# A trunk kernel's stick-breaking attention: beta stays in PSUM, the mask becomes a matmul, and GpSimd takes subtractions

## The chip, the cores and the metric

The kernel runs as one program on one core of a Trainium2 chip. The metric is the device time of one execution in microseconds (us). The engines are named as the profile names them: PE is TensorE's matmuls and PEld its weight loads, DVE is VectorE, ACT is ScalarE, POOL is GpSimd, SP is SyncE, which issues the DMAs. "L582" is line 582 of the kernel before.

## What is computed

A trunk of two layers over 1024 frames of width 1024, in float32. Layer 0 mixes stick-breaking attention (8 heads of 64) and a pooling mixer, layer 1 is gated linear attention, and each is followed by a gated MLP with a causal convolution of width 3. The change touches layer 0's attention and what surrounds it:

```python
def even_mixer(h, w_in, q_gain, k_gain, pool_w, pool_scale, w_out):
    proj = h @ w_in
    q, k, v, xb = jnp.split(proj, [SB_WIDTH, 2 * SB_WIDTH, 3 * SB_WIDTH], axis=-1)
    q = rms_norm(q.reshape(b, s, SB_HEADS, SB_HEAD_DIM), q_gain)
    k = rms_norm(k.reshape(b, s, SB_HEADS, SB_HEAD_DIM), k_gain)
    o_a = stick_breaking_attention(q, k, v)
    o_b = multiscale_pool(xb, pool_w, pool_scale)
    return jnp.concatenate([o_a, o_b], axis=-1) @ w_out

# stick_breaking_attention: A[t,s] = beta_ts * prod_{s<j<t}(1 - beta_tj), s < t
    z = einsum(q_blk, kh) * dh ** -0.5
    visible = key_pos < q_pos
    log_fail = where(visible, log_sigmoid(-z), 0)
    later = (cumulative sum of log_fail from the right, without the element itself)
    weights = where(visible, exp(log_sigmoid(z) + later), 0)
    out = weights @ v
```

So with beta = sigmoid(z), a weight is beta times the product of (1 - beta) over all later visible keys.

## The kernel before

Activations lie transposed, 128 features by 1024 frames to a tile. Every float32 operand of a matmul is split into a rounded part hi (fp32r, made by ScalarE's copy) and a rest lo (fp32r, made by a subtraction); `mm3` (L122) then does hi x hi, hi x lo and lo x hi. So every tile costs a ScalarE copy and a subtraction before TensorE can use it: `load_split` (L102) for weights, with the subtraction on VectorE or, with `eng=G`, on GpSimd; `stack` (L443) for a head's q and k; `pool_out` (L487, ph and pl) and `split_h` (L509, mh and ml) for what goes into the output projection.

**Attention.** For each of 4 pairs p of heads, each head a, and each block i of 128 queries, the keys up to the diagonal are cut into chunks of 512: one *unit* is a block of queries against one chunk, of 128, 256, 384 or 512 columns. The unit with the diagonal comes first, and its neighbour to the left continues its product. 96 units in all, 64 with the diagonal. A unit goes through these steps:

- `scores` (L558): two matmuls (L562, L563) put z into a PSUM bank "z". ScalarE makes pt = sigmoid(-z), that is 1 - beta (L567), and bt = beta (L569), both into SBUF. In a diagonal unit GpSimd sets the column after the last to 1 (L571), and two selects (L573) set the masked part of the last 128 columns of pt to 1 and of bt to 0.
- `weights` (L576): VectorE runs a multiplying scan over pt from right to left (L582; its second operator is a bypass, so what stands as the second input is read and not used), and multiplies bt by pt moved by one (L584).
- `transpose` (L586): TensorE transposes bt, 128 columns at a time (L590), into a bank "t"; ScalarE and VectorE empty it into the parts hi (L598) and lo (L599).
- `outputs` (L601), once per two blocks of queries: matmuls with the values (L609, L611) into a bank "d", which ScalarE (L614) and VectorE (L617) empty.

**Order.** TensorE's order is written out by hand (L664 to L695). Step s issues the scores of unit s+2, the weights of unit s+1, and the transposes of unit s. Between them a `Filler` (L143) issues other matmuls, by a planned time per column (`seg`, `RATES`): projections of the next pair's q and k (`qk_prep`, L365), pooling (`pool_in`, `pool_out`), values, and last, in segment (3,0), the first part of the output projection (`out_first`, L519). A generator that yields None ends the current fill, so that a few steps pass before its next matmul. `out_first` splits the six inputs listed in `first`, with two None each, and then multiplies with all six. The queues of the other engines are ordered by the framework, which plans with a model of its own, and then run strictly in that order. At the start of each segment `stack` prepares the head that comes one segment later; for the first two heads it runs right before the attention.

**PSUM.** Eight banks: two each for the names lin (projections), z, t and d, taken in turns. `qk_prep` puts the statistics of q and k (L376) and two transposed row scales (L431) into d.

## Time and profile before

| | us |
|---|---|
| median of 3 runs (2330.53 to 2331.79) | 2330.87 |
| the profiled execution | 2332.11 |
| its span, first to last instruction | 2330.1 |
| PE busy in it | 2230.3 (96%) |
| DVE busy | 1691.2 (73%) |
| ACT busy | 1024.7 (44%) |
| POOL busy | 468.6 (20%) |

Section 2 of the page cuts the span into 40 slices and gives each engine's busy share in tenths; PEclk is the clock granted to TensorE, where 9 stands for 90% or more. In a list of waits, a row reads: the engine and line that waited, the engine and line that released it, total us, times, longest us. In a list of one line's instructions the three numbers are the shortest, median and longest in ns. In a timeline a row gives start and duration in us, and in brackets the idle time before it and what ended it; "x4" is four merged instructions. Matmul durations overlap, so TensorE's pace is read from the distance of their starts.

The attention stage runs from about 66 to 452 us. The first MLP follows it.

### The profile page before, as it was taken

How to read it: one execution, taken by the hardware profiler on the slowest of the kernel's cores; microseconds unless marked ns; L12 is line 12 of the kernel's file. 1: busy time of each engine (PE TensorE's matmuls, PEld its weight loads, DVE VectorE, ACT ScalarE, POOL GpSimd, SP SyncE). 2: the span in 40 equal slices, each digit the busy share in tenths (PEclk: the TensorE clock that was granted, in tenths of full speed). 3: DMA queues.
4: the chain of work that ended last, by engine and by line, in shares of the span. 5: the costliest groups of instructions: out<-in, count | busy, mean ns of one | idle time of the engine just before them, and what ended most of it. 6: DMA issues, size and time to landing. Idle time of an engine off the chain costs nothing.

```text
span 2330.1 us, 27466 instructions
## 1 busy us (share of the span) xinstructions
PE 2230.3 (96%) x10560; PEld 1832.4 (79%) x10560; DVE 1691.2 (73%) x2236; ACT 1024.7 (44%) x1492; POOL 468.6 (20%) x422
## 2 busy tenths in 40 slices
PE   8989988989999999999998999999899999999999
PEld 7778767767888887888886888787688888878887
DVE  5687797698999998744445545557999999986543
ACT  6556665464444444312146343627544444442210
POOL 1352462041111111422020000003211111124210
PEclk9999989999999999999999999999899999999999
DMA  4001112222222224522001111112122222254211
GB/s 140 19 19 31 38 32 101 68 100 64 82 84 82 84 85 137 204 103 91 10 23 43 37 37 37 46 38 90 64 89 84 82 82 82 82 199 163 92 53 73
DMA packets 51427, 178.53 MB, mean 77 GB/s; under 512 B 5968, under 2 KB 6608, under 8 KB 51296
## 3 DMA queue, kind: packets, MB, share of 16 engines
q1 hardware_dynamic: 51296, 176.78, 23.0%
q8 instruction: 83, 1.36, 0.2%
q14 instruction: 48, 0.39, 0.1%
HBM read 140.06 MB, written 36.70 MB: 76 GB/s over the span
## 4 chain that ended last, share of the span: by engine, by line
PE 80%; DVE 11%; ACT 4%; issue 3%; DMA 1%; POOL 1%; SPq 0%; DVEq 0%; POOLq 0%; ACTq 0%
PE lin L783 15%; PE z L783 10%; PE lin L127 5%; PE lin L129 5%; PE t L783 5%; PE d L783 5%; PE lin L131 5%; PE z L127 2%; PE z L129 2%; PE z L131 2%; PE t L127 2%; PE t L129 2%; PE t L131 2%; PE d L129 2%; PE d L127 2%
## 5 line engine op out<-in xcount | busy, mean ns | idle before, releaser
L113 ACT CAST whi<-wraw 128x1024 fp32r<-128x1024 f32 (+4 forms) x108 | 107.5, 997 | 359.2 <-PE d L129 229.3
L941 POOL TENSOR_TENSOR c<-c 128x1024 f32<-128x1024 f32 x44 | 108.1, 2458 | 756.4 <-ACT c L940 756.4
L801 DVE TENSOR_TENSOR u<-u,rstd_bc 128x512 f32<-128x512 f32 x168 | 167.1, 996 | 2.8
L114 DVE TENSOR_TENSOR wlo<-wraw,whi 128x1024 fp32r<-128x1024 f32 (+3 forms) x96 | 138.0, 1438 | 40.5 <-ACT whi L113 39.6
L970 POOL TENSOR_TENSOR act<-a,act 128x1024 fp32r<-128x1024 f32 x40 | 107.8, 2703 | 217.7 <-ACT act L969 210.8
L846 ACT ACTIVATE c<-u,prm 128x1024 f32<-128x1024 f32 x88 | 109.3, 1245 | 84.8 <-DVE u L801 73.8
L582 DVE TENSOR_TENSOR_SCAN pt<-pt 128x128 f32<-128x128 f32 (+3 forms) x96 | 99.9, 1041 | 37.9 <-POOL pt L573 28.6
L127 PE MATMUL lin<-h_hi,whi 128*128 128x512 f32 x304 | 119.6, 432 | 7.0 <-ACT whi L113 7.0
L783 PE MATMUL d<-T,a 128*128 128x512 f32 x504 | 121.1, 389 | 0.0
L849 DVE SCALAR_TENSOR_TENSOR c<-u,prm,c 128x1022 f32<-128x1022 f32 x88 | 115.3, 1312 | 0.1
L847 DVE SCALAR_TENSOR_TENSOR c<-u,prm,c 128x1023 f32<-128x1023 f32 x88 | 112.3, 1278 | 2.8 <-ACT c L846 2.7
L722 DVE TENSOR_TENSOR x<-x,t 128x512 f32<-128x512 f32 x97 | 66.4, 684 | 66.1 <-PE t L131 66.0
L129 PE MATMUL lin<-h_lo,whi 128*128 128x512 f32 x304 | 112.3, 407 | 0.3
L131 PE MATMUL lin<-h_hi,wlo 128*128 128x512 f32 x304 | 111.5, 406 | 0.0
L783 PE MATMUL lin<-T,s12h 128*128 128x512 f32 x336 | 105.8, 396 | 5.8 <-ACT tm L816 5.8
L783 PEld LDWEIGHTS d<-T,a 128*128 128x128 f32 x504 | 94.6, 188 | 19.6
L762 ACT CAST s12h<-s 128x1024 fp32r<-128x1024 f32 x42 | 44.2, 1053 | 146.1 <-PE lin L783 146.1
L783 PE MATMUL z<-blk,s34h 128*128 128x512 f32 x336 | 105.7, 395 | 2.8 <-DVE u L832 2.8
L722 DVE TENSOR_TENSOR x<-x,d 128x512 f32<-128x512 f32 x97 | 66.3, 684 | 56.8 <-PE d L131 56.7
L783 PE MATMUL lin<-blk,whi 128*128 128x512 f32 x336 | 106.6, 399 | 0.0
L783 PE MATMUL z<-blk,s12h 128*128 128x512 f32 x336 | 105.8, 396 | 0.0
L783 PE MATMUL t<-blk,whi 128*128 128x512 f32 x336 | 103.7, 390 | 0.0
(388 smaller groups left out, 6526.7 us busy)
## 6 DMA issues: line engine op xcount, KB each, us to landing
wraw<-in_wup SPq DMA_DIRECT2D x46, 512.0 KB, 3.6
act<-c SPq DMA_DIRECT2D x44, 512.0 KB, 2.6
wraw<-in_wdn SPq DMA_DIRECT2D x44, 512.0 KB, 3.7
raw_g<-in_wup SPq DMA_DIRECT2D x42, 512.0 KB, 3.6
a<-act SPq DMA_DIRECT2D x40, 512.0 KB, 4.4
xs<-x SPq DMA_DIRECT2D x16, 512.0 KB, 2.6
x<-xs SPq DMA_DIRECT2D x16, 512.0 KB, 5.0
x<-in_xT SPq DMA_DIRECT2D x8, 512.0 KB, 6.0
```

The lines of the kernel that those rows point to most:

```text
L114: (eng or V).tensor_tensor(lo[:, cs], raw[:, cs], hi[:, cs].bitcast(F32), op=ALU.subtract)
L127: PE.matmul(out[i], wh, ah[i], start=first, stop=False)
L129: PE.matmul(out[i], wh, al[i], start=False, stop=False)
L131: PE.matmul(out[i], wl, ah[i], start=False, stop=last)
L722: V.tensor_tensor(x[m][:, cs], x[m][:, cs], pss[i], op=ALU.add)
L783: PE.matmul(ps, w, m, start=first and k == 0 and n == 0, stop=k == 3 and n == 2, skip_group_check=True)
L801: V.tensor_tensor(dst, dst, rstd_bc[:, cs], op=ALU.mult)
L846: S.activation(c, u, AF.Identity, scale=pcol(b + 2), bias=pcol(b + 3))
L847: V.scalar_tensor_tensor(c[:, 1:], u[:, :T - 1], pcol(b + 1), c[:, 1:], op0=ALU.mult, op1=ALU.add)
L849: V.scalar_tensor_tensor(c[:, 2:], u[:, :T - 2], pcol(b), c[:, 2:], op0=ALU.mult, op1=ALU.add)
L941: G.tensor_tensor(ca, ca, cg, op=ALU.mult)
L970: G.tensor_tensor(t[1], a32, t[0].bitcast(F32), op=ALU.subtract)
```

## The change

- **PSUM banks.** One name per bank, and a table says which use takes which banks in turn. Outside the attention it is as before, two for each of lin, z, t, d. During the attention z has three and d one. `qk_prep`'s statistics and row scales use t instead of d, except for the first pair's, before the attention.
- **Mask.** Two constants are made at the start: minus 1e30 on a diagonal, and a triangle of ones. In a diagonal unit a third matmul adds their product to the last 128 columns of z; the sigmoids then give 1 and 0 there. The two selects and the memset on GpSimd go; ScalarE copies the 1 into pt's extra column.
- **beta in PSUM.** The second sigmoid writes over z in its bank. The scan's second, unused input is now that bank, and the product reads beta from it and writes bt anew in SBUF (2 buffers instead of 3).
- **Subtractions.** VectorE's subtractions in `stack` (kl, qs), `pool_out` (pl) and `split_h` (two loaded and all but the last computed input) go to GpSimd.

```diff
-    psum = ctx.enter_context(tc.tile_pool(name="psum", bufs=2, space=PSUM))
+    psum = ctx.enter_context(tc.tile_pool(name="psum", bufs=1, space=PSUM))
...
+    turns = {}
+
+    def share_out(**uses):
+        turns.clear()
+        turns.update({u: itertools.cycle(b) for u, b in uses.items()})
+
     def bank(tag):
-        return psum.tile([P, 512], F32, tag=tag, name=tag)
+        return psum.tile([P, 512], F32, tag=f"bank{next(turns[tag])}", name=tag)
+
+    share_out(lin=(0, 1), z=(2, 3), t=(4, 5), d=(6, 7))
...
+    tri = etile("pw", F32, 528)[:, 0:P]
+    G.affine_select(out=tri, in_=ones, compare_op=ALU.is_ge, fill=0.0,
+                    base=0, pattern=[[1, P]], channel_multiplier=-1)
+    S.copy(later, tri)
+    S.activation(nbig, ident, AF.Copy, scale=-MASK)
...
-            st = bank("d")
+            st = bank("t" if start is None else "d")
...
-            bc = bank("d")
+            bc = bank("t" if start is None else "d")
...
-        V.tensor_sub(kl[r], kg[r], kh[r].bitcast(F32))
-        V.tensor_sub(qs[o], qg[r], qs[r].bitcast(F32))
+        G.tensor_tensor(kl[r], kg[r], kh[r].bitcast(F32), op=ALU.subtract)
+        G.tensor_tensor(qs[o], qg[r], qs[r].bitcast(F32), op=ALU.subtract)
...
-            V.tensor_sub(pl, ob[:, cs], ph.bitcast(F32))
+            G.tensor_tensor(pl, ob[:, cs], ph.bitcast(F32), op=ALU.subtract)
...
-            return load_split(o_d[k - NPAIR], hpool, ("h", "h"), nb=16)
+            return load_split(o_d[k - NPAIR], hpool, ("h", "h"), nb=16, eng=G)
...
-        V.tensor_sub(ml, src, mh.bitcast(F32))
+        (V if k == NPAIR - 1 else G).tensor_tensor(ml, src, mh.bitcast(F32), op=ALU.subtract)
...
-        z = bank("z")[:, 0:u.n]
+        n, first_ = u.n, u.above is None
+        u.z = z = bank("z")[:, 0:n]
...
-        PE.matmul(z, lq, kl[:, u.k0:u.k1], start=False, stop=True)
+        PE.matmul(z, lq, kl[:, u.k0:u.k1], start=False, stop=not first_)
+        if first_:
+            PE.matmul(z[:, n - P:n], nbig, later, start=False, stop=True)
...
-        u.bt = bt = etile("bt", F32, 512, 3)
-        S.activation(bt[:, 0:n], z, AF.Sigmoid, scale=qsc[:, 0, col:col + 1])
-        if u.above is None:
-            G.memset(pt[:, n:n + 1], 1.0)
-            for d_, fill in ((pt[:, n - P:n], 1.0), (bt[:, n - P:n], 0.0)):
-                G.affine_select(out=d_, in_=d_, compare_op=ALU.is_gt, fill=fill,
-                                base=0, pattern=[[-1, P]], channel_multiplier=1)
+        if first_:
+            S.copy(pt[:, n:n + 1], ones[:, 0:1])
+
+        S.activation(z, z, AF.Sigmoid, scale=qsc[:, 0, col:col + 1])
...
-        V.tensor_tensor_scan(pr, pr, pr, 1.0 if first_ else u.above.pt[:, 0:1],
+        V.tensor_tensor_scan(pr, pr, z[:, ::-1], 1.0 if first_ else u.above.pt[:, 0:1],
                              op0=ALU.mult, op1=ALU.bypass)
-        V.tensor_tensor(bt[:, 0:n], bt[:, 0:n], pt[:, 1:n + 1], op=ALU.mult)
+        u.bt = etile("bt", F32, 512, 2)
+        V.tensor_tensor(u.bt[:, 0:n], z, pt[:, 1:n + 1], op=ALU.mult)
...
+    share_out(lin=(0, 1), z=(2, 3, 6), t=(4, 5), d=(7,))
...
+    share_out(lin=(0, 1), z=(2, 3), t=(4, 5), d=(6, 7))
```

The last two lines stand right before and right after the attention's loop.

## The prediction

> **What bounds the kernel now.** I read the page's slices first, to find where TensorE is not full; then busy times by stage; then what TensorE waited for in the two bad stages; then one stall instruction by instruction.

> ```profile
> PE   8989988989999999999998999999899999999999
> ...
> DVE  5687797698999998744445545557999999986543
> ...
> PEclk9999989999999999999999999999899999999999
> ```
> One slice is 58.3 us. TensorE is full nearly everywhere; the change touches only the attention stage, slices 2 to 8 (about 64 to 455 us), where PE drops to 8 three times, the clock to 8 once, and VectorE (DVE) rises to 9 there. What lies behind 460 us keeps its instructions, so the sum concerns these stages:

> ```profile
> 64.00:76.00 12.00, 7.38 (x22) 5.54 (x21) 5.05 (x6) 5.28 (x10) 7.71 (x11) 0.72 0.00 0
> 76.00:320.00 244.00, 225.90 (x1319) 193.98 (x1318) 190.23 (x325) 157.41 (x306) 99.18 (x169) 0.97 0.09 28
> 320.00:390.00 70.00, 54.04 (x243) 44.25 (x242) 62.01 (x85) 39.06 (x69) 34.58 (x48) 0.83 0.26 90
> 390.00:452.00 62.00, 62.00 (x328) 52.39 (x328) 41.18 (x65) 26.30 (x50) 7.93 (x22) 1.00 0.16 50
> ```
> The columns are stretch, length, busy time of PE, PEld, DVE, ACT, POOL, granted clock, DMA share and GB/s. In 76 to 320 TensorE idles 244.0 - 225.9 = 18.1 us, and a clock of 0.97 costs 225.9 x 0.03 = 6.8 us more. In 320 to 390 it idles 16.0 us and the clock costs 54.0 x 0.17 = 9.2 us. From 390 to 452 it idles not at all: nothing can be won there except by less TensorE work. What TensorE waited for, first in 76 to 320, then in 320 to 390 (total, times, longest):

> ```profile
> PE t L590 <- DVE atl L599: 7.5, 2, 3.8
> PE d L611 <- DVE atl L599: 3.4, 4, 2.0
> ```
> ```profile
> PE d L611 <- DVE atl L599: 9.2, 4, 4.0
> PE t L590 <- DVE atl L599: 5.5, 2, 4.5
> ```
> So 10.9 of 18.1 us, and 14.7 of 16.0 us, end when VectorE's L599 has emptied a transpose bank. VectorE is late, not slow by itself; one such stall shows why (GpSimd, VectorE, TensorE):

> ```profile
> 153.88 2.51 POOL L114 TENSOR_TENSOR wlo<-wraw,whi 128x1024 fp32r<-128x1024 f32 x1
> ```
> ```profile
> 152.91 1.28 DVE L584 TENSOR_TENSOR bt<-bt,pt 128x512 f32<-128x512 f32 x1
> 154.22 3.25 DVE L451 TENSOR_TENSOR qs<-qg,qs 64x1024 fp32r<-64x1024 f32 x1
> 157.50 0.69 DVE L599 TENSOR_TENSOR atl<-t,ath 128x512 fp32r<-128x512 f32 x1
> ```
> ```profile
> 158.25 1.12 PE L590 MATMUL t<-ident,bt 128*128 128x128 f32 x4 [3.82 <-DVE atl L599]
> ```
> L451 stands ahead of the urgent L599 in VectorE's queue. It starts at 154.22, GpSimd's subtraction ends at 156.39, and 1.08 us later L451 is done: it got through only after GpSimd. TensorE lost 3.82 us.

> **The change part by part.** Which VectorE instructions does GpSimd stretch? Shortest, median and longest in ns:

> ```profile
> L584 DVE TENSOR_TENSOR bt<-bt,pt x96: 270/680/1522, 71.7 to 430.9; 128x512 f32<-128x512 f32 x48, 128x128 f32<-128x128 f32 x16, 128x256 f32<-128x256 f32 x16, 128x384 f32<-128x384 f32 x16
> ```
> ```profile
> L582 DVE TENSOR_TENSOR_SCAN pt<-pt x96: 417/1210/2285, 71.1 to 429.5; 128x512 f32<-128x512 f32 x48, 128x128 f32<-128x128 f32 x16, 128x256 f32<-128x256 f32 x16, 128x384 f32<-128x384 f32 x16
> ```
> ```profile
> L494 DVE TENSOR_TENSOR pl<-o_b,ph x8: 658/666/1518, 141.4 to 382.6; 128x512 fp32r<-128x512 f32 x8
> ```
> ```profile
> L464 DVE TENSOR_TENSOR o_b<-lin,rstd_bc x8: 659/674/692, 115.3 to 333.4; 128x512 f32<-128x512 f32 x8
> ```
> L494, with both inputs in SBUF, reaches 1518 ns; L464, with one in PSUM, never passes 692. The scan and the product become of L464's kind, so I take them at their short durations, never stretched. Reading PSUM costs 674 - 666 = 8 ns by these rows, under 2 us over 192 instructions.

> [...] The two rows above show 8 ns, and I go by them.

> VectorE also loses the subtractions. GpSimd's work by rows:

> ```profile
> L573 POOL TENSOR_SCALAR_AFFINE_SELECT bt<-bt 128x128 f32<-128x128 f32 x64 | 37.6, 588 | 4.7 <-ACT bt L569 4.2
> L573 POOL TENSOR_SCALAR_AFFINE_SELECT pt<-pt 128x128 f32<-128x128 f32 x64 | 30.7, 480 | 138.1 <-ACT pt L567 117.8 <-PE t L590 11.6 <-PE lin L131 8.3
> ```
> ```profile
> L114 POOL TENSOR_TENSOR wlo<-wraw,whi x12: 1268/2387/3062, 7.1 to 285.6; 128x1024 fp32r<-128x1024 f32 x10, 128x512 fp32r<-128x512 f32 x2
> ```
> ```profile
> L450 DVE TENSOR_TENSOR kl<-kg,kh x8: 1216/1220/1999, 64.2 to 330.3; 64x1024 fp32r<-64x1024 f32 x8
> ```
> ```profile
> L451 DVE TENSOR_TENSOR qs<-qg,qs x8: 1218/1220/3255, 35.6 to 334.9; 64x1024 fp32r<-64x1024 f32 x8
> ```
> Removed from GpSimd: 128 selects, 68.3 us. Added: 16 subtractions for kl and qs, 7 in split_h, 8 halves in pool_out. At 2.39 us for 1024 columns and 1.27 for 512: 23 x 2.39 + 8 x 1.27 = 65 us (a 64-partition one may be anything from half of 2.39 to all of it; I take all, as L450 on 64 partitions costs VectorE the same 1.22 as 128). GpSimd's total stays, but in 2.4 us pieces. VectorE loses 23 x 1.22 + 8 x 0.67 = 33 us.

> *76 to 320.* No L450, L451 or L494 stands ahead of an L599, and nothing stretches. Of the 10.9 us of late L599 and the 6.8 us of clock behind the long stalls, 17.7 in all, I take back 16 (bounds 8 and 18): the four pl here may come up to 2.4 us late behind another subtraction, and TensorE waits for those at once. The other new subtractions queue ahead of GpSimd's weight splits, made one projection ahead (10.4 us by the planner), and of the next head's stack, needed one segment later, (452 - 66) / 8 = 48 us. That lead hides them; without it each would cost up to 2.4 us.

> *320 to 390.* Here GpSimd itself runs full:

> ```profile
> 320.00:361.00 41.00, 26.87 (x116) 21.70 (x115) 40.26 (x51) 25.94 (x46) 30.44 (x39) 0.75 0.21 67
> ```
> ```profile
> 320.00:361.00 41.00, 10.74 (x14) 0.75 0.21 67
> ```
> ```profile
> 320.00:361.00 41.00, 5.47 (x4) 0.75 0.21 67
> ```
> The second row is the selects of L573, the third VectorE's L516. GpSimd after: 30.4 - 10.7 + 6 x 2.39 (split_h for the six of `first`) + 2 x 2.39 (stack) + 2 x 1.27 = 41 us, of the stretch's 41. What remains was itself stretched by VectorE; allowing 4 us for that, 37. VectorE falls from 40.3 by 5.5 + 6 (two loaded splits, stack, pool_out) to under 29; TensorE's own work is 26.9 x 0.75 = 20. out_first's matmuls need all six splits, so the wait for L599 turns into one for GpSimd: I take back 4, and 2 behind 361, together 6 (bounds 0 and 21, the latter if pool_in's chain steps aside).

> [...]

> *Mask.* 64 matmuls of 128 columns, each with a weight load. Successive starts of such:

> ```profile
> 332.67 0.22 PE L562 MATMUL z<-kh,qs 128*128 128x128 f32 x1
> 332.73 0.28 PE L563 MATMUL z<-kl,qs 128*128 128x128 f32 x1
> 332.84 0.30 PE L590 MATMUL t<-ident,bt 128*128 128x128 f32 x1
> ```
> 0.06 to 0.11 us: 3.8 to 7.0 us, all on TensorE's path; I take +6, nearer the second, as L563 too follows an accumulating matmul.

> *Longer chain.* The scan now reads beta, so it waits for the second sigmoid and, in a unit with the diagonal, for a one-column ScalarE copy between the two; ScalarE's queue behind them waits with it. A 512 unit (z at 412.6; its transposes are the last row):

> ```profile
> 413.68 0.68 ACT L569 ACTIVATE bt<-z,qsc 128x512 f32<-128x512 f32 x1
> ```
> ```profile
> 415.21 0.69 DVE L584 TENSOR_TENSOR bt<-bt,pt 128x512 f32<-128x512 f32 x1
> ```
> ```profile
> 421.25 0.60 PE L590 MATMUL t<-ident,bt 128*128 128x128 f32 x4
> ```
> The product ends at 415.9, 5.3 us before TensorE asks. The wait adds 0.68, and the copy no more than another 0.68; queued behind the scan is at most an L599 of the unit before. Cost 0, while 5 us of cover stand; without any, 96 x 0.68 + 64 x 0.68 = 109 us. ScalarE, 157 of 244 busy, takes the 64 copies. The in-place sigmoid holds its z bank until the product; with three such banks TensorE needs one again only after it has transposed that product: 0.

> *Banks.* qk_prep's two statistics and two row-scale transposes move from d to t: 4 turns x 3 preps, each a possible wait of the next transposes for VectorE. +2 (0 to 12 x 3.8, the longest such wait above). One d bank instead of two: outputs come every second to fourth unit; 0.

> *Start.* The first head's stack:

> ```profile
> 64.37 3.96 POOL L452 TENSOR_SCALAR kh<-kh 64x1024 fp32r<-64x1024 f32 x2 [15.17 <-ACT kh L448]
> ```
> ```profile
> 69.50 0.47 PE L563 MATMUL z<-kl,qs 128*128 128x128 f32 x1 [2.77 <-POOL kl L453]
> ```
> After: a subtraction of 2.39 and two copies of 1.98 from 64.4 give 70.8 instead of 69.5, or 2.4 later if the second head's subtraction goes between: +1 (-1, if the copies run unstretched, to +4). The mask's constants fall into idle time like the 15.17 us before this row: 0. SP issues the same DMAs in the same places.

> **Sum.** -16 - 6 + 6 + 2 + 1 = -13. The profiled execution took 2332.1 us (span 2330.1), the runs' median is 1.2 below; so 2319.1 profiled, **2318 us**.

> **Rivals.** *GpSimd gets its splits done in time:* 320 to 390 gives 20, and 76 to 320 gives 18: -18 - 20 + 6 + 1 = -31, 2300 us. For: pool_in's chain isn't urgent, and VectorE no longer slows GpSimd. Against: 37 us of work for it. *The port is not freed:* the scan still writes and reads SBUF; if it collides as before, only the moved instructions count, -8 - 4 + 6 + 2 + 1 = -3, 2328 us. L464's 692 speaks against. *The t banks become the narrow place:* in the three preps the transposes wait behind statistics that VectorE reads late. At half of the longest wait, 12 x 1.9 = 23 us in place of 2: 2339 us, slower. It decides once these turns cost over 15 us. For: t L590 is already where TensorE waits. Against: VectorE becomes freer.

> **Numbers.** Forecast 0.50, splits in time 0.20, port not freed 0.13, t banks 0.17. A measurement here can tell about 0.2%, 4.7 us, from no change: below 2326.2 is faster, above 2335.5 slower. Hence 0.69 faster (a little of the forecast ends inside), 0.14 the same, 0.17 slower. The forecast alone runs from 2308 to 2328; the range from 2300, the second case, to 2334, where part of the t-bank case is left out.

> **What would show it.** Right: scan and product never above 1.4 and 0.75 us; no TensorE wait above 2 us on L599 in 76 to 320, with clock 0.99; in the last pair's start a wait on GpSimd's ml or pl; 64 mask matmuls spaced by 0.1 us. Wrong: L582 still reaching 2 us, TensorE waiting for t in the preps, or no wait on GpSimd and out_first starting 15 us earlier.

## The result and the profile after

The changed kernel takes 2344.22 us (median of 4 runs, 2343.41 to 2344.77), the kernel before beside it 2331.33 us (4 runs): 1.0052 times as long, 95% interval 1.0040 to 1.0064. It is 13 us slower where 13 us faster were forecast, and 10 us above the range. The profiled execution spans 2343.1 us against 2330.1. In run 11 below, one execution took 2438.95 us where the other four took 2337 to 2343; its numbers are those of the four.

The page's slices, then busy times by stage (columns as above) of the changed kernel:

```profile
PE   8899988989999999999998999999799999999999
...
DVE  5476776698999998745445545557999999986543
...
PEclk9898999999999999999999999999999999999999
```
```profile
64.00:76.00 12.00, 4.01 (x14) 2.17 (x13) 1.80 (x4) 5.18 (x8) 8.83 (x6) 0.74 0.00 1
76.00:320.00 244.00, 233.10 (x1335) 202.03 (x1334) 160.63 (x304) 157.40 (x343) 67.73 (x45) 0.93 0.09 28
320.00:390.00 70.00, 54.30 (x276) 45.49 (x276) 52.34 (x81) 42.08 (x85) 42.30 (x36) 0.88 0.26 90
390.00:452.00 62.00, 61.52 (x321) 51.78 (x320) 40.39 (x65) 28.67 (x60) 2.40 (x1) 0.99 0.13 38
```
VectorE got its relief: 160.6 us busy in 76 to 320 instead of 190.2. TensorE idles 10.9 us there instead of 18.1, and yet gains nothing: its clock fell from 0.97 to 0.93, which costs 233.1 x 0.07 = 16.3 us where 6.8 were lost before. Two slices now show clock 8, the second (58 to 117 us) and the fourth.

Where the time went can be read from the start of the same matmul in both traces, since TensorE's order is unchanged but for the 64 mask matmuls. Each trace is one execution, and one such lag carries a few us of chance: run 1 below has the same program up to 207 us, and its lag at 163 us is 0 where it is 4.4 here. The lag of the changed kernel in us, beside what the forecast's terms make of it (the mask's 6 us spread over the heads):

| at (time before) | lag | forecast for the step |
|---|---|---|
| 48 (in the prologue) | +2.0 | 0 |
| 80 (first head runs) | +5.8 | +1 |
| 104 (first statistics passed) | +10.8 | not given |
| 163 | +4.4 | not given |
| 225 (first pool output passed) | +11.3 | not given |
| 320 | +8.3 | -9 |
| 390 | +5.3 | -14 |
| 465 | +7.6 | -13 |
| 1180 (gated part begins) | +7.5 | -13 |
| behind 1700 | +13.0 | -13 |

So 5.8 us are lost before the heads run, 2.5 between 80 and 320, 3.0 are won from 320 to 390, 2.2 are lost up to 1180, and 5.5 behind 1180, where nothing was changed but the turns of the banks. Three of these places show their cause at once.

*Prologue.* GpSimd, VectorE and TensorE of the changed kernel:

```profile
35.24 4.85 POOL L471 TENSOR_TENSOR qs<-qg,qs 64x1024 fp32r<-64x1024 f32 x2 [23.05 <-ACT qs L469]
```
```profile
38.09 3.08 DVE L252 TENSOR_TENSOR kl<-ident,rstd_tok 128x1024 f32<-128x1024 f32 x1
```
```profile
42.37 0.43 PE L369 MATMUL lin<-whi,h_hi 128*128 128x256 f32 x1 [0.69 <-DVE sc L402]
```
The two qs subtractions of the first pair were 2.47 us of VectorE before. On GpSimd they end at 40.09, and L252, two SBUF inputs, ends 1.08 us after that: 3.08 us for 1.23 before. It is the collision that the prediction read at 154 us, now in a place where it stands ahead of the statistics. Five other runs with qs on GpSimd have it too, with 0.4 to 2.3 us of lag at 48.

*First stack.*

```profile
66.72 2.33 POOL L470 TENSOR_TENSOR kl<-kg,kh 64x1024 fp32r<-64x1024 f32 x1 [15.16 <-ACT kh L468]
69.15 1.04 POOL L472 TENSOR_SCALAR kh<-kh 64x1024 fp32r<-64x1024 f32 x1
70.27 2.34 POOL L470 TENSOR_TENSOR kl<-kg,kh 64x1024 fp32r<-64x1024 f32 x1
72.69 1.04 POOL L472 TENSOR_SCALAR kh<-kh 64x1024 fp32r<-64x1024 f32 x1
73.81 2.16 POOL L473 TENSOR_SCALAR kl<-kl 64x1024 fp32r<-64x1024 f32 x2
```
```profile
70.24 0.47 PE L583 MATMUL z<-kh,qs 128*128 128x128 f32 x1 [3.23 <-POOL kh L472]
74.91 0.47 PE L584 MATMUL z<-kl,qs 128*128 128x128 f32 x1 [4.19 <-POOL kl L473]
```
The second head's subtraction (and its kh copy) go between, the case that the prediction named at 2.4 later; with the copy it is 3.4, and TensorE waits 7.4 us here, against 4.6 before (2.8 of them on L453, as the prediction shows).

*Statistics on t.* VectorE's queue and TensorE of the changed kernel, then the same statistics before:

```profile
95.28 0.69 DVE L600 TENSOR_TENSOR_SCAN pt<-pt,z 128x256 f32<-128x256 f32 x1 [2.11 <-ACT z L593]
95.88 0.27 DVE L618 TENSOR_TENSOR atl<-t,ath 128x128 fp32r<-128x128 f32 x1
```
```profile
96.20 2.77 PE L399 MATMUL t<-ind,sq 128*128 128x2 f32 x16 [1.37 <-DVE atl L618]
```
```profile
88.87 1.84 PE L379 MATMUL d<-ind,sq 128*128 128x2 f32 x16
```
The scan waits for the second sigmoid, L618 stands behind the scan, the t bank behind L618, and the statistics behind the t bank. The wait is only 1.37 us. More is lost behind it, where the clock falls; first the changed kernel, then the same 8 us before:

```profile
96.00:104.00 8.00, 7.80 (x29) 6.92 (x30) 3.58 (x9) 1.89 (x5) 0.00 (x0) 0.57 0.25 68
```
```profile
88.50:96.50 8.00, 8.00 (x48) 6.98 (x47) 6.36 (x14) 4.99 (x12) 3.53 (x7) 1.00 0.26 69
```
Without a wait the 16 small matmuls leave the clock at 1.00; behind a wait of 1.37 us it was 0.57 for 8 us, 29 matmuls in place of 48 by the rows' count.

### The profile page after: what moved, and what is told of

It is laid out like the page before. It is cut to its first block, busy times and chain, and to the rows that moved or that the text cites. A ratio compares the mean times of both kernels' runs of the same rounds, so it can differ in the third digit from the quotient of the medians.

```text
span 2343.1 us, 27351 instructions
## 1 busy us (share of the span) xinstructions
PE 2242.7 (96%) x10624; PEld 1844.4 (79%) x10624; DVE 1650.6 (70%) x2205; ACT 1030.0 (44%) x1558; POOL 444.2 (19%) x262
## 4 chain that ended last, share of the span: by engine, by line
PE 83%; DVE 9%; ACT 4%; issue 2%; DMA 1%; POOL 1%; SPq 0%; DVEq 0%; ACTq 0%; POOLq 0%
PE lin L804 14%; PE z L804 10%; PE lin L137 6%; PE lin L139 5%; PE lin L141 5%; PE t L804 5%; PE d L804 5%; PE z L137 2%; PE z L139 2%; PE z L141 2%; PE t L137 2%; PE t L139 2%; PE t L141 2%; PE d L141 2%; PE d L139 2%; PE d L137 2%
## 5 line engine op out<-in xcount | busy, mean ns | idle before, releaser
L124 DVE TENSOR_TENSOR wlo<-wraw,whi 128x1024 fp32r<-128x1024 f32 (+3 forms) x94 | 139.8, 1487 | 41.5 <-ACT whi L123 37.1
L600 DVE TENSOR_TENSOR_SCAN pt<-pt,z 128x128 f32<-128x128 f32 (+3 forms) x96 | 93.1, 970 | 73.6 <-ACT z L593 72.8
```

Source lines behind the costliest of these rows:

```text
L124: (eng or V).tensor_tensor(lo[:, cs], raw[:, cs], hi[:, cs].bitcast(F32), op=ALU.subtract)
```

## The experiments

Each ran beside the kernel before, whose median stayed within 2331.9 to 2332.6 us; ratios are to that, with their 95% interval. The changed kernel was not run again beside them, so that a difference to its 2344.22 us is good to about 1 us only: the kernel before moved by 1.3 us from one group of runs to another.

**1. The turns of the banks put back.** The old pool did not alternate strictly. In the built program it gave the same bank twice in a row at eleven places, from 207 us on; the change's cycles never do, but for the single d bank.

```diff
     def bank(tag):
-        return psum.tile([P, 512], F32, tag=f"bank{next(turns[tag])}", name=tag)
+        if (tag, taken[tag]) not in AGAIN:
+            shown[tag] = next(turns[tag])
+        taken[tag] += 1
+        return psum.tile([P, 512], F32, tag=f"bank{shown[tag]}", name=tag)
```

> The changed kernel with one thing put back: at the eleven places where the framework's two-buffer ring of the kernel before handed out the same bank twice in a row (the first pool product, the two FFN starts, one statistics bank near 1190 us, the second state product of three heads of the gated part), the same bank is handed out twice here too; everywhere else the banks alternate as in the changed kernel. Theory A (strict alternation makes TensorE wait for a slow reader at these places): about 6 us come back of the 13, nearly all behind 1160 us, where the lag of TensorE's work grew from 7.5 to 13.0 us: 2338 us, and the two waits on vl in the gated part (1.14 us, with half clock behind) become waits on state (0.75 us). Theory B (the growth behind 1160 us is only the phase in which the clock drops, and belongs to no edit): nothing systematic comes back, 2342 to 2346 us, and steps of about 1.9 us move to other places.

Measured: 2339.52 us, ratio 1.0029 (1.0018 to 1.0040), 4.7 below the changed kernel. A second state product of the gated part waited, in the changed kernel and then in this one, for:

```profile
L1176 PE MATMUL d<-vh,kdh x4: 381/480/578, 1467.0 to 1472.1; 64*128 64x256 f32 x4
its engine sat idle before it (us, times) until:
  DVE vl L1079: 1.1, 1
```
```profile
L1183 PE MATMUL d<-vh,kdh x14: 381/381/383, 1461.4 to 1479.0; 64*128 64x256 f32 x14
its engine sat idle before it (us, times) until:
  DVE state L1188: 0.7, 1
```
At 0.7 us the matmuls keep 381 ns; at 1.1 us they go up to 578. The steps of 1.9 us at 1460 and 1.5 at 1568 are gone. They stand in the traces of all six kernels with strict turns (the changed one, runs 2, 3, 4, 5 and 9) and in none of the other ten. But the total proves less than it seems: 4.5 us of lag were already back by 120 us, ahead of the first repeated bank at 207. Behind the same waits there the clock fell less: 1.00 against 0.79 behind the one at 42 us, 0.79 against 0.57 behind the one ahead of the first statistics.

**2. The strict turns alone, on the kernel before.**

```diff
+    turns = {u: itertools.cycle((0, 1)) for u in ("lin", "z", "t", "d")}
     def bank(tag):
-        return psum.tile([P, 512], F32, tag=tag, name=tag)
+        return psum.tile([P, 512], F32, tag=f"{tag}{next(turns[tag])}", name=tag)
```

> The kernel before with nothing changed but that its four pairs of banks alternate strictly instead of going by the framework's ring; no other edit of the change is in it. Theory A: the same places wait, and the kernel before becomes about 6 us slower, 2337 us, with the steps behind 1160 us. Theory B: 2331 us, within 1.5 us.

Measured: 2339.62 us, ratio 1.0029 (1.0018 to 1.0041), 7.7 us slower by this alone, and so the total is theory A's. The trace shows only a part of it where a bank's turn differs. But for a passing 3 us at 207, the lag stays within 0.5 us up to 350, rises by 3.3 there, and again in steps of 1.5 to 1.9 at 1190, 1460, 1568 and 1670. No turn differs at 350 or 1190, and the step at 1190 comes up in kernels with the old turns as well (runs 6, 8 and 14). That much of theory B, steps which belong to no edit, is true too.

**3. The stacks back on VectorE.**

```diff
-        G.tensor_tensor(kl[r], kg[r], kh[r].bitcast(F32), op=ALU.subtract)
-        G.tensor_tensor(qs[o], qg[r], qs[r].bitcast(F32), op=ALU.subtract)
+        V.tensor_sub(kl[r], kg[r], kh[r].bitcast(F32))
+        V.tensor_sub(qs[o], qg[r], qs[r].bitcast(F32))
```

> The changed kernel with the subtractions of the key and query stacks (kl and qs) back on VectorE, eight heads. Theory C (the start pays 2.4 us for the vector engine slowed beside GpSimd at 38 us and 3.1 us for the order on GpSimd at 66 to 75 us, and later heads are hidden): the lag at 80 us falls from 5.8 to 0 to 1 us, the other heads move by less than 2 us, 2338 to 2340 us. Theory D (VectorE is what the middle heads wait for, and 38 us of subtractions go back on it): the start is regained but 76 to 320 us lose 5 to 10 us, 2340 to 2348 us.

Measured: 2338.44 us, ratio 1.0021 (1.0012 to 1.0030), 5.8 below the changed kernel. The lag at 80 us is 1.2 instead of 5.8, and at 320 it is 2.3 instead of 8.3. Theory C: the heads in the middle lose no more than before, though VectorE has 16 x 1.22 = 20 us more to do (the 38 us expected of it are GpSimd's time for the same, 16 x 2.39).

**4. Statistics on d, and the old shares.**

```diff
-            st = bank("t" if start is None else "d")
+            st = bank("d")
-            bc = bank("t" if start is None else "d")
+            bc = bank("d")
-    share_out(lin=(0, 1), z=(2, 3, 6), t=(4, 5), d=(7,))
```

> The changed kernel with the statistics and row scales of the later pairs back on the d banks, and so with z on two banks and d on two for the whole of it. Theory E (a statistics product on a t bank waits for the last reader of transposes and leaves TensorE at half clock behind it, 4.6 us at 96 us and about 2 us at each of four to five more places): 8 to 12 us come back between 80 and 320 us, 2332 to 2336 us. Theory F (the third z bank carries the longer hold of the scores, so that two banks make the scores wait): what comes back is eaten, and waits of z on the product L603 appear, 2344 us or more.

Measured: 2331.06 us, ratio 0.9993 (0.9984 to 1.0002): 13.2 us come back, the most of any single step. This undoes three things together (t, the third z bank, the single d bank), which the runs 9 to 12 take apart.

**5. pl back on VectorE.**

```diff
-            G.tensor_tensor(pl, ob[:, cs], ph.bitcast(F32), op=ALU.subtract)
+            V.tensor_sub(pl, ob[:, cs], ph.bitcast(F32))
```

> The changed kernel with one subtraction back on VectorE: pl of the pool outputs (two 128x512 pieces per output, four outputs). Theory H (pl queues on GpSimd behind the h splits, the head stacks and the pooling chain; TensorE waits 6.6 us for it in three places and runs at half clock behind them): 5 to 7 us come back, the 4.5 us wait at 212 to 220 us and the 3 us at 342 us are gone, 2338 us. Theory I (behind pl the next wait is as late, since ph and the chain feed the same product): 0 to 2 us, 2342 to 2344 us.

Measured: 2336.36 us, ratio 1.0018 (1.0008 to 1.0027), 7.9 below the changed kernel, in which pl stood so at 345 us:

```profile
343.12 2.34 POOL L124 TENSOR_TENSOR wlo<-wraw,whi 128x1024 fp32r<-128x1024 f32 x1
345.42 1.26 POOL L514 TENSOR_TENSOR pl<-o_b,ph 128x512 fp32r<-128x512 f32 x1
```
```profile
346.74 0.80 PE L139 MATMUL lin<-pl,whi 128*128 128x512 f32 x1 [4.49 <-POOL pl L514]
```
L124 is the split of one of the loaded inputs of the output projection, which TensorE first uses behind 361 us. It stands ahead of the urgent pl: L451 ahead of L599 again, with GpSimd in VectorE's place.

**6 and 7. What is left of the change.** Run 6 undoes 1, 3, 4 and 5 together (banks as rings of two); run 7 puts the h splits on VectorE as well, so that only beta in the bank and the mask on TensorE remain.

```diff
-            return load_split(o_d[k - NPAIR], hpool, ("h", "h"), nb=16, eng=G)
+            return load_split(o_d[k - NPAIR], hpool, ("h", "h"), nb=16)
-        (V if k == NPAIR - 1 else G).tensor_tensor(ml, src, mh.bitcast(F32), op=ALU.subtract)
+        V.tensor_sub(ml, src, mh.bitcast(F32))
```

> Beta in the scores' bank, the mask on TensorE and the h splits on GpSimd stay; the banks, the statistics and the row scales are those of the kernel before (two-buffer rings, statistics on d), and kl, qs and pl are back on VectorE. If what the runs so far gave back adds up (4.7 for the turns, 13.2 for statistics and banks, 5.8 for the stacks, about 5 for pl, all from 2344.2 us): 2315 us, faster than the kernel before by 16 us, which is the gain forecast for 76 to 390 us without its costs. If the parts overlap (each gave back the same late scores): 2325 to 2331 us.

> As the run beside it, and the h splits on VectorE too, so that only beta in the scores' bank and the mask on TensorE are left of the change. If VectorE's 12 splits of 2.39 us on GpSimd are a gain at 320 to 390 us, as the prediction held: 5 to 8 us slower than the run beside it, about 2322 us. If GpSimd's slow two-input subtraction is late there as well: the same within 2 us or faster.

Measured: run 6 2324.38 us, ratio 0.9966 (0.9955 to 0.9978), faster than both kernels; run 7 2332.32 us, 0.9999 (0.9990 to 1.0008). The h splits on GpSimd are worth 8 us in this company; beta and mask alone, with two z banks, nothing. Run 6 by stage, and its waits in 76 to 320:

```profile
76.00:320.00 244.00, 232.15 (x1378) 200.83 (x1377) 185.56 (x334) 163.64 (x354) 51.67 (x40) 0.97 0.09 28
320.00:390.00 70.00, 59.68 (x308) 49.76 (x307) 55.45 (x83) 42.84 (x89) 28.45 (x22) 0.93 0.30 103
```
```profile
PE z L576 <- DVE bt L596: 4.4, 4, 2.0
PE d L623 <- DVE atl L611: 2.2, 2, 1.9
...
PE t L602 <- DVE atl L611: 0.3, 1, 0.3
```
The waits on atl fell from 10.9 to 2.5 us, and 4.4 us came up as a wait of the scores for the product (L596) that now frees their bank. The parts of runs 1, 3, 4 and 5 give 31.5 us by themselves and 19.8 together, so they overlap.

**8. All subtractions moved, and nothing else.** The kernel before with kl, qs, pl and the h splits on GpSimd by the lines of the change; the mask stays on GpSimd in SBUF.

```diff
-        V.tensor_sub(kl[r], kg[r], kh[r].bitcast(F32))
+        G.tensor_tensor(kl[r], kg[r], kh[r].bitcast(F32), op=ALU.subtract)
...
-            V.tensor_sub(pl, ob[:, cs], ph.bitcast(F32))
+            G.tensor_tensor(pl, ob[:, cs], ph.bitcast(F32), op=ALU.subtract)
```

> The kernel before with only the subtractions moved to GpSimd (kl, qs, pl, h splits), which still makes the mask in SBUF: banks, scan and statistics are untouched. If the moved subtractions cost by their place in GpSimd's queue, they cost more here, behind 128 mask selections: 10 us and more, 2342 us or above. If they relieve VectorE in the middle heads more than they cost: 2325 to 2331 us.

Measured: 2361.52 us, ratio 1.0124 (1.0110 to 1.0138), 29 us slower. From 30 to 390 us VectorE's scans waited 41.6 us, once 10.7, for the mask's selections (L573), which now stand behind the moved work; in the kernel before it was 25.4, at most 3.7. TensorE's waits for the products behind them rose from 1.3 to 11.5 us from 30 to 320. So much moved work does need the mask out of GpSimd's queue.

**9 and 10. One d bank.** Run 9 is the changed kernel with the first two edits of run 4 alone: three z banks and one d bank stay. Run 10 adds the turns of run 1 and kl, qs and pl on VectorE: it is run 6 with the third z bank taken from d.

```diff
-            st = bank("t" if start is None else "d")
+            st = bank("d")
-            bc = bank("t" if start is None else "d")
+            bc = bank("d")
```

> The changed kernel with its shares of banks (z on three, d on one bank), and only the statistics and row scales put back on d, which is one bank here. Theory E (the statistics wait on a t bank for the last reader of transposes, and TensorE runs at half clock behind them): most of the 13 us that came back with statistics and banks come back here too, 2332 to 2335 us. Theory J (it was d on one bank, by which each output waits for the reader of the one before, 6.5 us for atl's reader and 4.6 us for ath's): with more work on that one bank it gets no better, 2343 to 2350 us.

> As the run with the banks of before and kl, qs, pl on VectorE (2324.4 us), but z on three banks and d on one while the heads run; the turns repeat a bank where the ring of before does. Theory K (what was left of the gain there went to the scores, which with two banks wait 7.0 us for the product that now frees their bank): the waits of z on bt go, 2317 to 2320 us. Theory J (d on one bank costs the outputs as much): 2324 to 2330 us, with waits of d on the readers of d.

Measured: run 9 2341.53 us, ratio 1.0043 (1.0030 to 1.0056); run 10 2336.00 us, 1.0015 (1.0006 to 1.0024), 11.6 above run 6. Taking a bank from d for z removed the wait for the product and cost more than it gave, as long as the statistics lay on d.

**11. Statistics on t alone, on the kernel before.**

```diff
-            st = bank("d")
+            st = bank("t" if start is None else "d")
-            bc = bank("d")
+            bc = bank("t" if start is None else "d")
```

> The kernel before with one edit of the change and no other: the statistics and row scales of the later pairs on the t banks instead of d (z and d keep two banks each, every bank goes by the ring). Theory L (16 matmuls of 128x2 behind a bank that is still read leave TensorE at half clock, some 3 to 4 us at each of the six statistics of the later pairs): 10 to 20 us slower than the kernel before, 2342 to 2352 us, with the steps at 88 to 93, 107 to 112, 175 to 182, 193, 268 to 273 and 286 to 291 us. Theory M (the turn on t costs only its own wait, 1.4 us at most each): 0 to 6 us slower, 2332 to 2338 us.

Measured: 2341.33 us (four runs), ratio 1.0038 (1.0024 to 1.0052): 9 us by this edit alone, 6 to 12 by the interval. That is close under theory L's 10 to 20 us and above M's 0 to 6. Its waits are short:

```profile
L379 PE MATMUL t<-ind,sq 128*128 128x2 f32 x96 | 12.4, 257 | 3.5 <-DVE atl L599 3.0 <-ACT sq L373 0.4
```
Behind each the lag grows by more than the wait: 2.7 at 89 us, 2.5 at 181, 2.6 at 273, 0.9 at 293.

**12. Statistics on a z turn.** Run 10 with one edit, statistics only:

```diff
-            st = bank("d")
+            st = bank("z" if start is None else "d")
```

> The run with three z banks, one d bank and kl, qs, pl on VectorE (2336.0 us), with the six statistics of the later pairs taken from d and put on the third z turn; the row scales stay on d. Theory L (the statistics cost what stands behind their wait, whatever bank it is): on a bank whose last reader is two scores back they find it free, the steps at 90, 175, 265 and 283 us go, and 8 to 12 us come back, 2324 to 2328 us or better. Theory N (one d bank costs by its outputs, or a statistics product that takes a turn of z delays the scores as much): 2334 to 2340 us.

Measured: 2328.11 us, ratio 0.9985 (0.9976 to 0.9994), 7.9 below run 10. The statistics in run 10, then in run 12:

```profile
L406 PE MATMUL d<-ind,sq 128*128 128x2 f32 x96 | 12.7, 260 | 5.2 <-DVE o_pair L643 4.7 <-ACT sq L400 0.4
```
```profile
L406 PE MATMUL z<-ind,sq 128*128 128x2 f32 x96 | 11.4, 247 | 0.5 <-ACT sq L400 0.4
```
4.7 us less wait gave 7.9 us. Theory L holds: the price is that of a wait right before the statistics, whichever bank causes it, t or a single d. Run 12 is still 3.7 us above run 6; this is what is left of the exchange of a d bank for a z bank once the statistics are out of d's way.

**13 and 14. Splits without beta in the bank.** Run 13 is the kernel before with only the h splits on GpSimd. Run 14 is run 6 with beta's sigmoid written to SBUF (two bt buffers, as the mask's constants leave no room for the third: the pool would take 69.22 kB per partition, and 68.31 are left), so that run 14 differs from run 6 by:

```diff
-        S.activation(z, z, AF.Sigmoid, scale=qsc[:, 0, col:col + 1])
+        u.bt = etile("bt", F32, 512, 2)
+        S.activation(u.bt[:, 0:n], z, AF.Sigmoid, scale=qsc[:, 0, col:col + 1])
...
-        V.tensor_tensor_scan(pr, pr, z[:, ::-1], 1.0 if first_ else u.above.pt[:, 0:1],
+        V.tensor_tensor_scan(pr, pr, pr, 1.0 if first_ else u.above.pt[:, 0:1],
...
-        V.tensor_tensor(u.bt[:, 0:n], z, pt[:, 1:n + 1], op=ALU.mult)
+        V.tensor_tensor(u.bt[:, 0:n], u.bt[:, 0:n], pt[:, 1:n + 1], op=ALU.mult)
```

> The kernel before with the h splits on GpSimd (all but the one at the end of the heads) and nothing else. If the splits are a gain by themselves, as between the two runs with the banks of before (2332.3 and 2324.4 us): 2324 us. If they need GpSimd free of the mask selections, behind which they queue and whose masks then come late: 2332 to 2345 us.

> The mask on TensorE and the h splits on GpSimd, banks and all other subtractions as before, and beta in SBUF (two buffers, as there is no room for a third), read there by the product, the scan with its old second operand. If the scores' wait for their bank (7.0 us on bt in the run with beta in the bank, 2324.4 us) is where the gain went: the waits of z on bt are gone and it is 2316 to 2320 us. If the bank's relief of the vector operand (686 against 738 ns, 1258 against 1299 ns) and the free port are the gain: 2328 to 2334 us, and waits of TensorE on atl are back.

Measured: run 13 2338.68 us, ratio 1.0025 (1.0014 to 1.0035); run 14 2339.97 us, 1.0030 (1.0018 to 1.0042), 15.6 above run 6. The 512-wide scan and product in run 6, then in run 14:

```profile
L593 DVE TENSOR_TENSOR_SCAN pt<-pt,z 128x512 f32<-128x512 f32 x48 | 60.4, 1258 | 26.5 <-ACT z L586 26.2
L596 DVE TENSOR_TENSOR bt<-z,pt 128x512 f32<-128x512 f32 x48 | 33.0, 687 | 3.7 <-PE t L602 1.1
```
```profile
L594 DVE TENSOR_TENSOR_SCAN pt<-pt 128x512 f32<-128x512 f32 x48 | 64.5, 1344 | 14.3 <-ACT pt L582 13.8
L596 DVE TENSOR_TENSOR bt<-bt,pt 128x512 f32<-128x512 f32 x48 | 44.8, 934 | 10.6 <-ACT bt L587 9.2
```
So the splits on GpSimd paid 8 us with mask and beta both moved (runs 6 and 7), and cost 6 with neither moved (run 13). Which of the two they need, these runs do not show. Run 13's trace has 3.5 us of lag behind the splits (324 to 465 us), where TensorE waited 3.9 us for products (L584) and before not at all; but the scans' waits for the mask hardly rose (26.3 against 25.4 us from 30 to 390), so that a late mask is not seen as the cause there, as it is in run 8. Another 2.9 us of its lag come near 1680 us, far from any edit. In run 14 TensorE's waits on atl are back at 15.0 us in 76 to 320, and the product is stretched again (up to 2726 ns for 512 columns). But run 14 also lacks the third buffer, and ScalarE waited 35.7 us in the attention for the transposes before writing beta. How much of the loss is that stays open.

## Why the prediction was wrong, step by step

- **Stretching ends: right.** Shortest, median and longest in ns in the changed kernel:

```profile
L600 DVE TENSOR_TENSOR_SCAN pt<-pt,z x96: 402/1080/1281, 76.3 to 436.1; 128x512 f32<-128x512 f32 x48, 128x128 f32<-128x128 f32 x16, 128x256 f32<-128x256 f32 x16, 128x384 f32<-128x384 f32 x16
```
```profile
L603 DVE TENSOR_TENSOR bt<-z,pt x96: 272/616/693, 76.7 to 437.5; 128x512 f32<-128x512 f32 x48, 128x128 f32<-128x128 f32 x16, 128x256 f32<-128x256 f32 x16, 128x384 f32<-128x384 f32 x16
```
  The longest were 2285 and 1522 before; now they are inside the 1.4 and 0.75 us given. The PSUM operand itself cost nothing that the medians show: for 512 columns they are 1275 against 1279 and 691 against 692 ns. The means fell more (1258 against 1299, 686 against 738), as those of before hold the stretched instructions. The port of the recorded texts is the author's explanation of the stretching; the runs show the durations alone.
- **76 to 320, -16: failed.** TensorE's waits in the changed kernel:

```profile
PE t L399 <- DVE atl L618: 3.3, 4, 1.4
PE d L630 <- DVE atl L618: 2.5, 2, 2.2
...
PE t L609 <- DVE atl L618: 0.6, 1, 0.6
```
  The waits of t and d on L618 did fall from 10.9 to 3.1 us, the longest 2.2. But four waits of the statistics on L618 came up, and the clock that should have risen to 0.99 fell to 0.93. The step took back a clock loss behind long stalls; it did not see that short waits cost clock as well. Even without the costs found since, run 6 gained only 3.5 us by 320, with some 4 us of the mask inside.
- **Banks, +2: the step that failed most.** The bounds (0 to 46) held the truth, the value did not: 9 us measured alone (run 11). I let the next transposes wait behind the statistics; the rows show the reverse, the statistics waiting for the reader of the transposes. And I priced the turn by its wait, which was short, 3.0 us in all; with the clock behind it a turn cost some 2.5 us in three of four places. The third rival named these banks, and TensorE waiting for t in the preps was among the signs of being wrong, but it too had the transposes wait, 1.9 us for each of twelve turns.
- **One d bank, 0: too low.** With the statistics off d, as in the change, the exchange of a d bank for a z bank cost some 3.7 us net (run 12 against run 6). The 11.6 us of run 10 have the statistics on the single d bank, which the change does not.
- **Turns, not in the sum: failed.** The diff showed cycles in the place of a pool; I took both to alternate. 7.7 us alone (run 2), 4.7 when undone (run 1).
- **Start, +1 (to +4): mis-sized.** 5.8 us of lag at 80 us: 3.8 by the named order on GpSimd, and 2.0 behind a collision on L252 that the prediction didn't look for ahead of 64 us. Run 3, which undoes all eight stacks, also gave back 5.8 us.
- **pl, taken as hidden but for up to 2.4 us: mis-sized.** 4.5 us of wait in one place, 7.9 us in all (run 5).
- **320 to 390, -6: half right.** The lag fell by 3.0 there, with pl's 4.5 us wait inside, and a second one of 4.6 us that the forecast has nowhere: TensorE on ScalarE's ath (L617), behind a ScalarE that had stood 5.3 us for a load of weights. That load was issued at 345.49, when GpSimd's split had freed its buffer; no run tested this. In run 6 the lag fell by 9.0 in this stage, in run 7, with the h splits on VectorE, by 1.5. So these splits gained where pl was not behind them, though one of 1024 columns took GpSimd 2.42 us (L536 at 361.59) where VectorE's median before was 1.22 (L516).
- **Mask, +6: its spacing held.** Successive starts in the changed kernel, at full clock:

```profile
127.55 0.27 PE L584 MATMUL z<-kl,qs 128*128 128x128 f32 x1
127.66 0.28 PE L586 MATMUL z<-later,nbig 128*128 128x128 f32 x1
127.77 0.45 PE L137 MATMUL lin<-h_hi,whi 128*128 128x512 f32 x1
```
  0.11 us each, 7 us for 64.
- **Longer chain, 0: failed in one link.** The cover of 5 us was TensorE's; VectorE's own queue had none, and L618 stood behind a scan that waited 2.11 us for the second sigmoid.

## What to carry to other kernels

A moved wait is priced by what follows it: where a burst of small matmuls came next, a wait of about a microsecond cost one to five here. Before an instruction goes to the queue of a slower engine (2.42 against 1.22 us here), list what already stands ahead of it at each place, the prologue too; urgent and patient work on one queue lost here on both engines (3.82 us behind L451 on VectorE before, 4.49 us behind L124 on GpSimd after). And replacing an allocator by a fixed rotation is an edit of its own: compare which bank each tile gets.

## What the runs showed of the hardware

TensorE's granted clock fell behind waits as short as 0.5 to 1.4 us when small matmuls followed (0.57 over 8 us behind 1.37 us at 96 us, 0.79 behind 0.53 us at 184 us in the changed kernel), and stayed at 1.00 for the same 16 matmuls without a wait at all six places of the kernel before. Over the sixteen traces the clock of the 8 us from the start of the later pairs' statistics was below 0.95 in 23 of 28 places with a wait of 0.5 to 1.7 us, and in 16 of 68 without one. It is not the same each time. At 42 us the changed kernel and run 1, whose programs are the same up to there, both wait 0.7 us for sc; the 8 us behind, first of the one, then of the other:

```profile
42.00:50.00 8.00, 7.63 (x52) 7.67 (x53) 3.64 (x9) 3.10 (x7) 2.23 (x2) 0.79 0.24 70
```
```profile
42.00:50.00 8.00, 7.71 (x65) 7.74 (x66) 4.72 (x11) 3.43 (x8) 3.33 (x2) 1.00 0.26 70
```
Clock 0.79 and 2.0 us of lag in the one, 1.00 and 0.4 us in the other. Differences of one or two microseconds at one place therefore prove nothing here; the verdicts above rest on medians and on steps that several kernels repeat.
